# Sums of the seven-product scheme in the first token block: split operands added in PSUM by TensorE through identity weights, instead of by VectorE

## The chip, the cores and the metric

The kernel runs on one core of one Trainium2 chip. The metric is the device time of one execution in microseconds. Before the change three runs took 2962.57, 2964.04 and 2958.99 us, median 2962.57.

## The reference

One layer of a streaming encoder over 2048 prompt rows and 64 sample rows of width 1024: a normalised projection, a convolution and an attention in parallel, a gated merge, an output projection with a residual, then a normalised feed-forward with a residual. The change lies between the output projection and the feed-forward:

```python
x = x + gt1 * (merged @ p['w_o'])
h2 = rms_norm(x, p['norm2_g']) * (1 + sc2) + sh2
gate, up = jnp.split(h2 @ p['w_ffn_in'], 2, axis=-1)
x = x + gt2 * ((jax.nn.silu(gate) * up) @ p['w_ffn_out'])
```

`w_ffn_in` is 1024 x 5632; gate and up have 2816 columns each (22 tiles of 128, called f in the code).

## The kernel before, in words

Everything is float32 carried as two rounded parts, hi and lo (type `fp32r`): a product a*b is three matmuls, hi*hi, hi*lo, lo*hi (`mm3`). A `split` makes the parts: ScalarE (ACT) writes hi by a copy, VectorE (DVE) subtracts it from the source and writes lo.

The second half of the program goes through the token blocks `CBLOCKS`: rows 0 to 576, 576 to 1344, 1344 to 2112. For each block, `merge` makes the merged rows, TensorE (PE) multiplies them by `w_o` into PSUM tiles `pw` (two banks of 512 columns for each 128 rows), `residual` turns each row tile into operands of the feed-forward, and then the products with `w_ffn_in` follow (tiles `ps`, `product`), then those with `w_ffn_out` (tiles `pd`).

The products with `w_ffn_in` use a scheme with seven products in place of eight. The normalised rows, transposed, are cut into four: b11 and b21 are the two halves of the 1024 features for the first half of the block's rows, b12 and b22 the same for the second half. What is multiplied is b11, b21, b22 and the sums

- t3 = b22 - b12
- t1 = b12 - b11
- t2 = b22 - t1
- t4 = b21 - t2

each split into hi and lo. In the first block each half has 288 rows, so these matmuls have 288 columns.

`residual` is a generator, one for each row tile. For one tile of the second half it does: two products with the gate row and two additions of x on DVE (x1), a square with a row sum on ACT, a power on GpSimd (POOL), a scaled copy on ACT (`xn`), eight 128x128 transposes on PE into the tile's own two `pw` banks, eight scalings with shift (`kk` in 0 to 7; the first bank in place, the second into `xn`), by ACT where `kk % 3`, else by DVE; then the sums. There, b[0] is b12 in PSUM (first bank), b[1] is b22 in SBUF (`xn`), t is the second bank. DVE makes t = b22 - b12; subtracts b11 hi and b11 lo from b[0]; makes t = b22 - b[0]; then b[0] = b21 hi - t, + b21 lo. With the splits that is 11 DVE and 5 ACT instructions of 128x512 for a tile.

The row tiles of the first block are 0 (64 sample rows), 64, 192, 320 and 448. Its second chunk, with `last` true, has the tiles 320 and 448; below they are called A and B. `W.early` is true in the first block until its generators are drained.

Order of the work: a recorder (`Meter`, `Stream`) adds estimated nanoseconds for each engine (`Stream.add`) and pumps generators (lanes `turns` and `work`) by these estimates; the weights' splits go to POOL or DVE by them too. Behind it, a scheduler places the instructions of each engine in its queue. Every engine runs its queue in order. While A and B are turned into operands, PE has products that need only b11 and b21: for each of the first five f (`EARLY`) one with b11 (`first`) and one with b21 (`second`) of 12 matmuls each, kept in `early` after a silu. Then come, for f = 0, the products with t3, t2, t1, t4 and b22 in this order (`up`), which need every row tile. `W.get` hands out the weights, loaded by SP's DMA queue, summed by POOL (`ws`), split by ACT (`whi`) and DVE or POOL (`wlo`).

All instructions have line 102 (the recorder's call), so they are told apart by tiles: `pw` the banks of A and B, `b` the tiles b11, b21 and b22 (hi and lo), `t` the tiles t1 to t4, `xn` the normalised rows, `ps` a feed-forward product, `early`, `u`, `v` its kept results, `hid` the hidden rows, `whi`, `wlo` weights.

Of the kernel before, what the change touches and what calls it, by code (L numbers as in the profile page):

```python
# [9 lines left out]
F32R = mybir.dt.float32r  # L10
AF = mybir.ActivationFunctionType
ALU = mybir.AluOpType
# [65 lines left out]
def tile_chunks(lo, hi):  # L78

    tiles = token_tiles(lo, hi)  # L80
    t, n = tiles[(len(tiles) + 1) // 2 - 1]
    return [(lo, t + n), (t + n, hi)]
# [87 lines left out]
class Stream:  # L170
# [7 lines left out]
    def add(self, name, op, n, args, kw):  # L178
        if name == "pe":
            x = args[1]  # L180
            if op == "transpose":
                ns = 128 / 1.2
            elif x.dtype == F32:
                ns = max(n, 64) / (2.4 if "tile_position" in kw else 0.6)
            else:
                ns = (n if n >= 256 else 512) / 2.4
        elif name == "act":
            ns = 220 + 0.83 * n
        elif name == "pool":
            ns = 260.0 * n if ALU.pow in args else 60 + 2.25 * n  # L190
        else:
            fast = op in ("tensor_scalar", "tensor_copy")
            ns = 75 + n * (8.3 if op == "reciprocal" else 0.75 if fast else 1.04)
        self.load[name] = max(self.load[name], self.load["pe"]) + ns
# [423 lines left out]
def streaming_layer(ctx: ExitStack, tc: tile.TileContext, I, O):  # L618
# [1129 lines left out]
    def residual(pp, t, n, gt1, a, half, hs, free, last, i):  # L1748


        which = int(t < SMP)
        if W.early:
            x_t = quarter("x_t", 1, F32, (P, D))
            nc.sync.dma_start(x_t[:n], rows(x_p, x_s, t, n))
            x_t = [x_t[:, 512 * j : 512 * j + 512] for j in range(2)]
        else:
            x_t = [wk.tile([P, 512], F32, tag="ws", name="x_t", bufs=4) for _ in range(2)]
            for j in range(2):
                nc.sync.dma_start(x_t[j][:n], rows(x_p, x_s, t, n)[:, 512 * j : 512 * j + 512])
        yield  # L1760
        x1 = token_row("x1")
        for j in range(2):
            f = slice(512 * j, 512 * j + 512)
            if t < SMP:
                fold(pp[j], x1[:n, f])
            stream.after("dve", "pe")
            dve.tensor_tensor(pp[j][:n], pp[j][:n], gt1[which][:n, f], ALU.mult)
        hs["rows"] -= 1
        yield
        for j in range(2):  # L1770
            f = slice(512 * j, 512 * j + 512)
            dve.tensor_tensor(x1[:n, f], pp[j][:n], x_t[j][:n], ALU.add)
        free()
        yield stream.when("dve")
        xn = token_row("xn")
        ssq = wk.tile([P, 1], F32, tag="ssq", bufs=2)
        act.activation(xn[:n], x1[:n], AF.Square, accum_out=ssq[:n])
        nc.sync.dma_start(x1_d[t : t + n], x1[:n])
        yield stream.when("act")
        r = rsqrt_mean(wk, ssq[:n], n, 1, D, 4)  # L1780

        W.behind = lambda ins=gps.last.ins: tc.issue_after(ins)
        yield stream.when("pool")
        stream.after("act", "pool")
        act.activation(xn[:n], x1[:n], AF.Copy, scale=r)
        yield stream.when("act")

        pts = pp if last else [bank_of(Y[i % 2 * 2 + j], "pt") for j in range(2)]
        pts = [pt.rearrange("p (k n) -> p k n", k=4) for pt in pts]
        for kk in range(KT):  # L1790
            pe.transpose(pts[kk // 4][:, kk % 4, :n], xn[:n, kk * P : (kk + 1) * P], ident[:n, :n])
        cols_ = [pts[0], xn[:, 512:].rearrange("p (k n) -> p k n", k=4) if a + n > half else pts[1]]
        for kk in range(KT):
            g, k = divmod(kk, 4)
            A, B = A2[:, kk, which : which + 1], B2[:, kk, which : which + 1]
            h = cols_[g][:, k, :n]
            if kk % 3:
                stream.after("act", "pe")
                act.activation(h, pts[g][:, k, :n], AF.Identity, bias=B, scale=A)
            else:  # L1800
                stream.after("dve", "pe")
                dve.tensor_scalar(h, pts[g][:, k, :n], A, B, ALU.mult, ALU.add)
        hs["columns"] -= 1
        yield stream.when("dve", "act")
        for c, e, o in ((0, min(n, half - a), a), (max(0, half - a), n, max(0, a - half))):
            if c >= e:
                continue
            b = [x[:, :, c:e] for x in cols_]
            at = lambda name: [hs[name][j][:, :, o : o + e - c] for j in range(2)]
            as_f32 = lambda name: [x.bitcast(F32) for x in at(name)]  # L1810
            if a + c < half:
                for g in range(2):
                    split(*at("b%d1" % (g + 1)), b[g])
                    yield stream.when("dve")
                continue

            yield lambda: not hs["rows"]
            assert not hs["rows"]
            for name in ("t2", "t3", "t1", "t4", "b22"):
                if name not in hs:  # L1820
                    hs[name] = [quarter(name, 1) for _ in range(2)]
            t = pts[1][:, :, c:e]
            stream.after("dve", "act")
            dve.tensor_tensor(t, b[1], b[0], ALU.subtract)
            stream.after("act", "dve")
            act.activation(at("t3")[0], t, AF.Copy)
            act.activation(at("b22")[0], b[1], AF.Copy)
            for x in as_f32("b11"):
                dve.tensor_tensor(b[0], b[0], x, ALU.subtract)
            dve.tensor_tensor(at("t3")[1], t, as_f32("t3")[0], ALU.subtract)  # L1830
            dve.tensor_tensor(t, b[1], b[0], ALU.subtract)
            yield stream.when("dve")
            split(*at("t2"), t)
            split(*at("t1"), b[0])
            yield stream.when("dve")
            dve.tensor_tensor(b[0], as_f32("b21")[0], t, ALU.subtract)
            dve.tensor_tensor(b[0], b[0], as_f32("b21")[1], ALU.add)
            dve.tensor_tensor(at("b22")[1], b[1], as_f32("b22")[0], ALU.subtract)
            yield stream.when("dve")
            split(*at("t4"), b[0])  # L1840
            yield stream.when("act")

    c0, c1 = tile_chunks(*CBLOCKS[0])
    nxt = [first_gates, gate_columns(*c0, 1)]
    srcs = [src]
    W.last_phase(wk, sum_d)
    for s, (lo, hi) in enumerate(CBLOCKS):
# [4 lines left out]
        for i, (c0, c1) in enumerate(chunks):  # L1852
            m = [wk.tile([P, KT, CW // 2], F32R, tag=f"m{j}", name="m") for j in range(2)]
            merge(c0, c1, srcs[i], m, nxt, (lambda: srcs.append(load_mixed(*chunks[1], 1))) if len(srcs) == 1 else None)
            if c1 < hi:
                nxt = [gate_columns(c1, hi, ct) for ct in range(2)]
            else:
                turns.drain(groups[0], True)
            grp = [(t, n) for t, n in tiles if c0 <= t < c1]
            pss = [[row_bank(i, j) for j in range(2)] for i in range(len(grp))]  # L1860
            if not groups:
# [459 lines left out]
```

## Time and profile before

| what | value |
|---|---|
| runs | 2958.99, 2962.57, 2964.04 us |
| profiled execution, its own time | 2963.08 us |
| its span, first to last instruction | 2961.1 us |
| mean granted TensorE clock | 0.997 |
| PE busy | 2892.8 us (98%) |
| DVE busy | 2050.5 us (69%) |
| ACT busy | 1364.9 us (46%) |
| POOL busy | 1155.6 us (39%) |

Times in rows are microseconds from the start of the span. A row of a timeline has start, length, engine, line, operation, out<-in, size, count, and in brackets how long the engine stood idle ahead of it and what it waited for. Rows that follow each other on one engine overlap a little: an instruction starts before the one ahead of it has ended.

### The profile page before, as it was taken

What the parts mean: (1) busy time and instruction counts of PE and PEld (TensorE: products, weight loads), DVE (VectorE), ACT (ScalarE), POOL (GpSimd) and SP (SyncE); (2) the same over time, 40 slices, a digit from 0 to 9 for tenths busy, and PEclk for the clock granted to TensorE, in tenths of its full rate; (3) what the DMA queues carried; (4) which work ended last, traced back from release to release, by engine and by line L of the source; (5) the groups of instructions that cost most, each with busy time, mean ns of one, the idle gap of its engine ahead of it and who ended that gap; (6) DMA issues with size and microseconds to landing.
All of it is one profiled execution on the core that took longest, in us unless ns stands there. A gap on an engine that the chain in (4) does not pass through costs nothing. (4 is left out here: it accounts for less than half of the span.)

```text
span 2961.1 us, 44835 instructions
## 1 busy us (share of the span) xinstructions
PE 2892.8 (98%) x16181; PEld 2584.5 (87%) x16181; DVE 2050.5 (69%) x3662; ACT 1364.9 (46%) x2453; POOL 1155.6 (39%) x747
## 2 busy tenths in 40 slices
PE   8999899999999999989999999999999999999999
PEld 5899777787888788889999998999999999999998
DVE  5897687668857885477777746676666547566666
ACT  3345633661465257464443345444444345444442
POOL 1101310111011102454466452366666742465767
PEclk9999999999999999999999999999999999999999
DMA  9988889988987889885444786333333965323333
GB/s 319 316 290 294 281 286 308 279 260 274 300 275 224 278 251 286 277 284 169 152 153 143 252 262 232 100 113 95 112 122 108 325 229 185 97 95 112 115 103 128
DMA packets 467067, 628.04 MB, mean 212 GB/s; under 512 B 36196, under 2 KB 314584, under 8 KB 466845
## 3 DMA queue, kind: packets, MB, share of 16 engines
q1 hardware_dynamic: 452944, 606.11, 63.2%
q10 hardware_dynamic: 13901, 19.08, 1.8%
q8 instruction: 127, 2.08, 0.3%
q14 instruction: 95, 0.78, 0.1%
HBM read 476.53 MB, written 148.54 MB: 211 GB/s over the span
## 5 line engine op out<-in xcount | busy, mean ns | idle before, releaser
L102 PE MATMUL ps<-t,whi 128*128 128x384 f32 (+1 forms) x2112 | 504.4, 323 | 9.1 <-ACT t L102 2.7
L102 POOL TENSOR_TENSOR wlo<-wst,whi 128x1024 fp32r<-128x1024 f32 (+1 forms) x158 | 361.2, 2298 | 242.8 <-ACT whi L102 217.1
L102 ACT ACTIVATE whi<-wst 128x1024 fp32r<-128x1024 f32 (+1 forms) x266 | 259.0, 978 | 325.5 <-PE ps L102 142.9
L102 PE MATMUL ps<-b,whi 128*128 128x384 f32 (+1 forms) x1584 | 380.2, 325 | 4.5 <-ACT early L102 1.4
L102 PEld LDWEIGHTS ps<-t,whi 128*128 128x128 f32 x2112 | 369.6, 189 | 16.8 <-ACT u L102 3.1
L102 DVE SCALAR_TENSOR_TENSOR y<-u,wd,y 128x512 f32<-128x512 f32 (+1 forms) x480 | 369.3, 773 | 6.3
L102 PE MATMUL ps<-hh,whi 128*128 128x512 f32 (+2 forms) x992 | 360.9, 364 | 0.0
L102 DVE TENSOR_TENSOR acc<-acc,pd 128x512 f32<-128x512 f32 x482 | 322.5, 685 | 49.3 <-PE pd L102 46.8
L102 PE MATMUL ps<-hl,whi 128*128 128x512 f32 (+2 forms) x992 | 344.9, 348 | 0.0
L102 PE MATMUL ps<-hh,wlo 128*128 128x512 f32 (+2 forms) x992 | 344.5, 347 | 0.0
L102 PE MATMUL ps<-t,wlo 128*128 128x384 f32 (+1 forms) x1056 | 339.3, 322 | 0.0
L102 PE MATMUL pd<-whi,hid 128*128 128x512 f32 x912 | 297.2, 391 | 0.3 <-DVE acc L102 0.3
L102 PEld LDWEIGHTS ps<-b,whi 128*128 128x128 f32 x1584 | 276.4, 188 | 12.8 <-ACT early L102 3.1
L102 POOL TENSOR_TENSOR r<-t,mhalf 128x1 f32<-128x1 f32 (+2 forms) x68 | 84.3, 1241 | 448.5 <-DVE t L102 443.5
L102 PE MATMUL ps<-b,wlo 128*128 128x384 f32 (+1 forms) x792 | 255.8, 323 | 0.0
L102 ACT ACTIVATE pr<-pr,sm 128x640 f32<-128x640 f32 (+3 forms) x272 | 200.2, 747 | 109.0 <-DVE sm L102 106.3
L102 PEld LDWEIGHTS ps<-hh,wlo 128*128 128x128 f32 x992 | 186.3, 188 | 21.6
L102 DVE TENSOR_TENSOR wlo<-wst,whi 128x1024 fp32r<-128x1024 f32 (+1 forms) x108 | 135.9, 1262 | 97.7 <-ACT whi L102 94.9
L102 PEld LDWEIGHTS ps<-hh,whi 128*128 128x128 f32 x992 | 186.8, 188 | 18.5 <-issue 1.6
L102 PEld LDWEIGHTS pd<-whi,hid 128*128 128x128 f32 x912 | 171.1, 188 | 36.1 <-DVE acc L102 1.0
L102 PEld LDWEIGHTS ps<-hl,whi 128*128 128x128 f32 x992 | 187.1, 189 | 15.4 <-issue 1.4
L102 PEld LDWEIGHTS ps<-t,wlo 128*128 128x128 f32 x1056 | 199.2, 189 | 0.7
(229 smaller groups left out, 6292.0 us busy)
## 6 DMA issues: line engine op xcount, KB each, us to landing
whi<-w_din_h SPq DMA_DIRECT2D x72, 512.0 KB, 6.8
wlo<-w_din_l SPq DMA_DIRECT2D x72, 512.0 KB, 7.3
wst<-sum_d SPq DMA_DIRECT2D x131, 256.0 KB, 2.9
wfo<-in_w_ffn_out SPq DMA_DIRECT2D x64, 512.0 KB, 3.8
wmod<-in_w_ada SPq DMA_DIRECT2D x46, 512.0 KB, 9.3
sum_d<-ws SPq DMA_DIRECT2D x88, 256.0 KB, 2.1
wst<-in_w_ffn_in SPq DMA_DIRECT2D x85, 256.0 KB, 3.2
wst<-in_w_in SPq DMA_DIRECT2D x40, 512.0 KB, 7.6
```

The lines of the kernel that those rows point to most:

```text
L102: self.last = f(*args, **kw)
```

## The change

Only the tiles A and B of the first block are touched (`by_pe = last and W.early`). For them

- DVE no longer subtracts b11 from b[0], no longer makes t a second time, and no longer combines b21 with t: 5 DVE instructions of 128x512 less for a tile.
- PE adds instead, straight into the PSUM bank, with a 128x128 tile of weights that is the identity or its negative (`signs`) and the hi and the lo part as moving data, 512 columns: b[0] += -b11, t += b11 (so t becomes t2), t += -b21 (so t becomes -t4). That is 3 pairs, 6 matmuls, for a tile.
- t4 is read with the sign turned: hi by an ACT copy with scale -1, lo by one DVE scalar_tensor_tensor.
- The eight transposes of a tile are given as four to an accumulation group (start flag on the first, stop on the fourth), as matmuls with `is_transpose`.
- Of the eight scalings DVE makes four (kk even) and ACT four, before DVE three and ACT five.
- `signs` is made by two ACT copies of the identity ahead of A and B.
- `Stream.add` counts such a transpose as it counted one before.

```diff
-            if op == "transpose":
+            if op == "transpose" or kw.get("is_transpose"):
...
         which = int(t < SMP)
+        by_pe = last and W.early
...
-            pe.transpose(pts[kk // 4][:, kk % 4, :n], xn[:n, kk * P : (kk + 1) * P], ident[:n, :n])
+            dst, src = pts[kk // 4][:, kk % 4, :n], xn[:n, kk * P : (kk + 1) * P]
+            if by_pe:
+                pe.matmul(
+                    dst, src, ident[:n, :n], is_transpose=True, start=kk % 4 == 0, stop=kk % 4 == 3,
+                    skip_group_check=True,
+                )
+            else:
+                pe.transpose(dst, src, ident[:n, :n])
...
-            if kk % 3:
+            if kk % (2 if by_pe else 3):
...
             dve.tensor_tensor(t, b[1], b[0], ALU.subtract)
+            if by_pe:
+                def add(dst, sign, name):
+                    for x in at(name):
+                        pe.matmul(dst, signs[0][:, sign], x, start=False, stop=True, skip_group_check=True)
+
+                split(*at("t3"), t)
+                add(b[0], 1, "b11")
+                yield stream.when("dve")
+                add(t, 0, "b11")
+                split(*at("b22"), b[1])
+                yield stream.when("dve")
+                split(*at("t2"), t)
+                split(*at("t1"), b[0])
+                yield stream.when("dve")
+                add(t, 1, "b21")
+                yield stream.when("dve")
+                act.activation(at("t4")[0], t, AF.Copy, scale=-1.0)
+                stream.after("dve", "act")
+                dve.scalar_tensor_tensor(at("t4")[1], t, -1.0, as_f32("t4")[0], ALU.mult, ALU.subtract)
+                yield stream.when("act")
+                continue
...
+                if not s:
+                    signs.append(wk.tile([P, 2, P], F32R, tag="tg1", name="signs", bufs=2))
+                    for j in range(2):
+                        act.activation(signs[0][:, j], ident, AF.Copy, scale=1.0 - 2.0 * j)
```

What this does to the queues is seen in the order of the instructions. First DVE, before, from the first lo part of t3 to the second one. Tile A has the banks pw_13557 (b[0]) and pw_13558 (t) and the rows xn_13793, tile B pw_13559, pw_13560 and xn_13871; b11 is 12924 and 12925, b21 12926 and 12927.

```order
L102 TENSOR_TENSOR t3_13740<-pw_13558,t3_13739 128x4x128
L102 TENSOR_SCALAR pw_13559<-pw_13559,A2_173,B2_174 128x128
L102 TENSOR_TENSOR pw_13558<-xn_13793,pw_13557 128x512
...
L102 TENSOR_TENSOR t1_13742<-pw_13557,t1_13741 128x4x128
L102 TENSOR_TENSOR pw_13560<-xn_13871,pw_13559 128x512
L102 TENSOR_TENSOR pw_13557<-b21_12926,pw_13558 128x512
L102 TENSOR_TENSOR pw_13559<-pw_13559,b11_12924 128x512
L102 TENSOR_TENSOR pw_13557<-pw_13557,b21_12927 128x512
L102 TENSOR_TENSOR pw_13559<-pw_13559,b11_12925 128x512
L102 TENSOR_TENSOR t3_13740<-pw_13560,t3_13739 128x4x128
```

The same stretch of DVE with the change; A has now the banks pw_13560 and pw_13561, B pw_13562 and pw_13563, and t3 is 13736 and 13737.

```order
L102 TENSOR_TENSOR t3_13737<-pw_13561,t3_13736 128x4x128
L102 TENSOR_TENSOR t1_13739<-pw_13560,t1_13738 128x4x128
L102 TENSOR_SCALAR xn_13915<-pw_13563,A2_173,B2_174 128x128
L102 TENSOR_TENSOR wlo_14009<-ws_13992,whi_14008 128x512
L102 TENSOR_TENSOR t2_13735<-pw_13561,t2_13734 128x4x128
L102 TENSOR_TENSOR pw_13563<-xn_13915,pw_13562 128x512
L102 SCALAR_TENSOR_TENSOR early_13731<-tg_14001,ps_13842 128x288
L102 TENSOR_TENSOR b22_13743<-xn_13915,b22_13742 128x4x128
L102 SCALAR_TENSOR_TENSOR t4_13741<-pw_13561,t4_13740 128x4x128
L102 TENSOR_TENSOR t3_13737<-pw_13563,t3_13736 128x4x128
```

Between B's first subtraction (pw_13560, now pw_13563, from xn) and B's lo part of t3 stood four instructions on the banks of A and B, and now stand a silu's end, a lo part of b22 and A's lo part of t4.

PE before, where the last product with b21 ends and the first with t3 begins (the third row goes to another f):

```order
L102 MATMUL ps_13993<-b21_12927,whi_13770 128x288
L102 MATMUL ps_13993<-b21_12926,wlo_13771 128x288
L102 MATMUL ps_14058<-t3_13739,whi_13846 128x288
L102 MATMUL ps_14171<-t3_13739,whi_14039 128x288
L102 MATMUL ps_14058<-t3_13740,whi_13846 128x288
```

PE with the change: first a place among the products with b21, where A's third pair and B's first pair of additions stand, then the same end of the products as above.

```order
L102 MATMUL ps_13957<-b21_12926,whi_13718 128x288
L102 MATMUL pw_13561<-b21_12926,signs_13557 128x512
L102 MATMUL pw_13561<-b21_12927,signs_13557 128x512
L102 MATMUL ps_13957<-b21_12927,whi_13718 128x288
L102 MATMUL ps_13957<-b21_12926,wlo_13719 128x288
L102 MATMUL pw_13562<-b11_12924,signs_13557 128x512
L102 MATMUL pw_13562<-b11_12925,signs_13557 128x512
...
L102 MATMUL ps_14004<-b21_12926,wlo_13774 128x288
L102 MATMUL ps_14063<-t3_13736,whi_13849 128x288
L102 MATMUL pw_13563<-b11_12924,signs_13557 128x512
L102 MATMUL pw_13563<-b11_12925,signs_13557 128x512
L102 MATMUL ps_14063<-t3_13737,whi_13849 128x288
```

Four of the six pairs stand ahead of the first product with t3, B's second pair behind its first matmul, and B's third pair behind the first matmuls with t2.

Beyond this place the order differs up to the products of f = 8 of the first block (names aside): six splits of weights that DVE made are POOL's, and the first matmuls with `w_ffn_out` come a little earlier on PE. From there on the order is the same.

More of the change, by code (lines that the diff above doesn't have):

```diff
@@ L1841, in residual @@
             yield stream.when("act")
+    signs = []
     c0, c1 = tile_chunks(*CBLOCKS[0])
```

## The prediction

> **What bounds the kernel now.** The page first: the span, the busy shares, the shares of the chain that ended last.
>
> ```profile
> span 2961.1 us, 44835 instructions
> ...
> PE 2892.8 (98%) x16181; PEld 2584.5 (87%) x16181; DVE 2050.5 (69%) x3662; ACT 1364.9 (46%) x2453; POOL 1155.6 (39%) x747
> ```
>
> PE is the bound nearly everywhere: work on another engine counts only where PE stands and waits for it, and every matmul that is added costs its time unless PE would have stood there. So the next view is who PE waited for, from the end of the first block's output projection on (1285 to 1400 us).
>
> ```profile
> PE ps L102 <- ACT t L102: 2.7, 1, 2.7
> PE ps L102 <- DVE u L102: 1.9, 1, 1.9
> PE ps L102 <- DVE t L102: 1.7, 1, 1.7
> ```
>
> Two of the three are waits for the tiles t1 to t4, which the change makes in another way. How much time the place holds is seen in the view by stretches; its columns are the length, the busy time of PE, of its weight load, of DVE, ACT and POOL (with counts), the granted clock, and DMA.
>
> ```profile
> 1306.00:1314.00 8.00, 7.90 (x58) 7.67 (x58) 6.72 (x14) 8.00 (x21) 3.61 (x3) 1.00 1.05 402
> 1314.00:1319.20 5.20, 0.82 (x5) 0.35 (x3) 4.86 (x10) 3.57 (x8) 0.34 (x1) 0.92 0.97 340
> 1319.20:1324.70 5.50, 5.42 (x22) 5.42 (x23) 5.50 (x11) 1.60 (x3) 2.32 (x3) 0.50 0.54 184
> 1324.70:1328.30 3.60, 3.54 (x25) 3.31 (x24) 3.60 (x4) 1.53 (x3) 2.48 (x2) 0.94 0.26 98
> 1328.30:1330.00 1.70, 0.00 (x0) 0.00 (x0) 1.70 (x5) 0.22 (x1) 0.17 (x1) 1.00 0.56 176
> 1330.00:1340.00 10.00, 9.58 (x71) 9.38 (x72) 9.78 (x18) 4.51 (x7) 3.72 (x3) 1.00 0.77 245
> sum 34.00, PE 27.27 PEld 26.14 DVE 32.16 ACT 19.43 POOL 12.63; mean PE 4.54 PEld 4.36 DVE 5.36 ACT 3.24 POOL 2.10
> ```
>
> DVE is busy without a gap from 1314 on, and PE stands: 34.00 - 27.27 = 6.7 us idle. In the third stretch, just behind the long stand, the granted clock is 0.50; PE's 5.42 us there are worth 2.7 us at full clock, so 2.7 us more are lost. **The place holds 9.4 us in all.**
>
> **The place row by row.** PE's timeline (the last 288-column products with b11 or b21, then those with the sums):
>
> ```profile
> 1313.60 0.30 PE L102 MATMUL ps<-b,wlo 128*128 128x288 f32 x1
> ...
> 1313.99 0.29 PE L102 MATMUL ps<-b,wlo 128*128 128x288 f32 x1
> 1317.03 0.53 PE L102 MATMUL ps<-t,whi 128*128 128x288 f32 x2 [2.74 <-ACT t L102]
> 1319.28 0.61 PE L102 MATMUL ps<-t,whi 128*128 128x288 f32 x1 [1.72 <-DVE t L102]
> 1319.68 0.45 PE L102 MATMUL ps<-t,wlo 128*128 128x288 f32 x1
> ...
> 1320.40 0.45 PE L102 MATMUL ps<-t,wlo 128*128 128x288 f32 x1
> ...
> 1330.12 0.50 PE L102 MATMUL ps<-t,whi 128*128 128x288 f32 x2 [1.87 <-DVE u L102]
> ```
>
> Three matmuls take 0.39 us (1313.60 to 1313.99), 0.13 each; behind the wait 0.72 (1319.68 to 1320.40), 0.24 each. DVE at the same time, from A's first subtraction to B's t3:
>
> ```profile
> 1308.72 0.69 DVE L102 TENSOR_TENSOR pw<-xn,pw 128x512 f32<-128x512 f32 x1 [1.11 <-ACT xn L102]
> ...
> 1315.55 0.69 DVE L102 TENSOR_TENSOR pw<-xn,pw 128x512 f32<-128x512 f32 x1
> 1316.15 0.69 DVE L102 TENSOR_TENSOR pw<-b,pw 128x512 f32<-128x512 f32 x1
> 1316.75 1.89 DVE L102 TENSOR_TENSOR pw<-pw,b 128x512 f32<-128x512 f32 x3
> 1318.54 1.28 DVE L102 TENSOR_TENSOR t<-pw,t 128x512 fp32r<-128x512 f32 x2
> ```
>
> B's t3 was subtracted at 1315.55, and its lo part was made at 1318.54 only, behind four instructions with b11 and b21 (1316.15 to 1318.54, 2.4 us). Those four are what the change takes off DVE. One DVE instruction of 128x512 follows the next after 0.60 us (1316.15 to 1316.75).
>
> **What is added to PE.** No row of before shows an addition with identity weights. The nearest are the output projection's matmuls, of the same type and 512 columns:
>
> ```profile
> 1284.62 0.61 PE L102 MATMUL pw<-whi,m 128*128 128x512 f32 x2
> ...
> 1285.30 0.61 PE L102 MATMUL pw<-whi,m 128*128 128x512 f32 x2
> ...
> L102 PE MATMUL pw<-whi,m x528: 387/389/497, 1210.8 to 2463.9; 128*128 128x512 f32 x176
> ```
>
> Three of them take 0.68 us, 0.227 each, and one alone lasts 0.389. Twelve additions cost 12 x 0.227 = **2.7 us**, at the most 12 x 0.389 = 4.7, each standing alone behind a wait. Below nothing it can't be: they are more work on the bound engine. The transposes stay sixteen in number and size; their flags cost nothing.
>
> **When PE runs out of free work.** These rows carry what follows: PE's first product behind the transposes, a scaling and a copy on ACT, a lo part on DVE.
>
> ```profile
> 1306.00 0.53 PE L102 MATMUL ps<-b,whi 128*128 128x288 f32 x2
> L102 ACT ACTIVATE xn<-pw,B,A x24: 452/464/502, 1306.0 to 2482.5; 128x128 f32<-128x128 f32 x24
> L102 ACT ACTIVATE t<-pw x32: 576/597/644, 1309.4 to 2495.8; 128x512 fp32r<-128x512 f32 x32
> L102 DVE TENSOR_TENSOR t<-pw,t x32: 676/682/693, 1311.1 to 2496.4; 128x512 fp32r<-128x512 f32 x32
> ```
>
> Before, the free products end about 1314.1 (1313.99 + 0.13). Now four pairs stand among them, 8 x 0.227 = 1.8 us: they end about 1315.8, if no addition waits.
>
> **Does one wait?** A's first pair stands behind some 18 products counted from 1306.0, at 1308.9; it needs A's first subtraction, which before ended at 1308.72 + 0.69 = 1309.4 and now about 1308.5, because ACT has one scaling less for A. A's second pair, 9 products and a pair later, starts near 1310.5 and is in PSUM at 1311.1; it needs A's lo part of t3, at 1310.2. B's subtraction now waits on a loop over three engines: A's second pair (1311.1), ACT's hi of t2 (0.60, ACT being busy until 1311.4: 1312.0), ACT's last scaling of B behind it (0.46: 1312.4), DVE's subtraction (0.69: 1313.1 to 1313.4). That is still more than 2 us ahead of before, 1315.55 + 0.69 = 1316.2. A's third pair needs A's lo part of t2, near 1312.8, and PE is there near 1312.7; B's first pair follows at 1313.6.
>
> **The waits for t3 and t2.** B's hi of t3 has b22's hi, an `early` copy and A's t4 ahead on ACT: 1314.1 to 1314.7. Its lo part on DVE follows A's t4: 1314.9 to 1315.6. PE asks for them at 1315.8. **The waits of 2.74 and 1.72 us close, with 0.2 us to spare, and with no long stand there is no half clock.** B's second pair then runs from 1315.9; hi of t2 is there at 1317.1, lo at 1317.9; PE, with 11 products of t3 (1.5 us) between, asks for them at 1317.8 and 1318.4. Two instructions that no row shows: the lo part of t4 is now a scalar_tensor_tensor reading PSUM. Its nearest rows are 0.68 for the lo parts above and 0.77 for this:
>
> ```profile
> L102 DVE SCALAR_TENSOR_TENSOR y<-u,wd,y 128x512 f32<-128x512 f32 (+1 forms) x480 | 369.3, 773 | 6.3
> ```
>
> I take 0.69: 0.1 at the most for each tile. The two ACT copies that make `signs` (0.46 each at the most, by the scalings) fall where PE works on the output projection and no wait of PE is listed after 1285 that they could lengthen; nothing. The scalings alternate between ACT and DVE more often, which may cost a hand-over of some 0.1 us each; they lie in the 0.9 us that A gains.
>
> **What is late next.** PE's products with t1 wait until DVE has taken `u` from their bank, the third wait (1.87). From B's first subtraction to `u` DVE needed 1329.53 - 1315.55 = 14.0 us for 21 instructions; now there are 14. Seven at 0.60 to 0.69 are 4.2 to 4.8 us, so `u` starts 9.2 to 9.8 behind 1312.7, at 1321.9 to 1322.5, where PE asks for it at 1321.5 (21 products behind the last pair) and gets it 0.44 later. Weights' splits stand in between, and these rows show what they can cost:
>
> ```profile
> 1324.89 1.54 DVE L102 TENSOR_TENSOR wlo<-ws,whi 128x512 fp32r<-128x512 f32 x1
> ...
> 1329.53 0.44 DVE L102 TENSOR_TENSOR u<-ps,early 128x288 f32<-128x288 f32 x1
> ...
> 1324.60 1.28 POOL L102 TENSOR_TENSOR ws<-ws,wup 128x512 f32<-128x512 f32 x1 [1.20 <-DVE wlo L102]
> ```
>
> The split took 1.54 us beside a sum of weights on POOL, 0.69 elsewhere; it ended 0.55 behind POOL's end. Such hits are in the 14.0 us, and one more or less moves `u` by 0.9. Behind that, the first matmul into `pd`, which now comes earlier, waits for `hid`, for which DVE has a split of 1024 columns ahead. Together these waits are between 0 and 2.5 us (1.0 and 1.5). I take 0.6, nearer to nothing, because the stretch of before up to `u` holds two such hits already and PE's demand comes 2 to 3 us later than DVE would be there without them.
>
> [...]
>
> **What cannot follow.** The weights are bound by DMA up to 1319: POOL's sum for f = 1 waits for a store,
>
> ```profile
> 1318.87 1.28 POOL L102 TENSOR_TENSOR ws<-wfo,ws 128x512 f32<-128x512 f32 x1 [9.18 <-DMA sum_d<-ws]
> ...
> 1340.00:1400.00 60.00, 60.00 (x369) 54.69 (x368) 46.13 (x78) 26.83 (x50) 26.04 (x18) 1.00 0.49 157
> ```
>
> and it will wait as long with the change. Its split is first used with b22 of f = 1, about 1333, so some 10 us are there. In the 60 us behind the place PE is busy without a gap, DVE has 14 us to spare and POOL 34; the six splits that go from DVE to POOL (some 1.3 to 2.6 us each) find room, and I cost the later order at nothing. Were POOL late, the wait would be PE's and start at a wait for `wlo`, which PE never had before.
>
> **The sum**, against the profiled execution's own 2963.08 us: -9.4 (idle and half clock) + 2.7 (additions) + 0.6 (waits left) = -6.1, so 2957.0. The median of the runs is 0.5 lower; for it I forecast 2962.57 - 6.1 = **2956.5 us**. Bounds: all waits closed, the short starts behind them too (four times some 0.3 us), -9.4 - 1.2 + 2.7 = -7.9; additions at 0.389 and waits of 2.5, -9.4 + 4.7 + 2.5 = -2.2.
>
> **The rivals.**
>
> *All closes.* DVE's `u` and `hid` are in time and the short starts go too: -7.9, so 2954.7. For it: PE asks late for everything. Against it: steps 0.2 us wide.
>
> *The half clock was this execution's own.* The 2.7 us come from a clock that halved once, behind 5 us of near idle. The runs lie 5 us apart (2958.99 to 2964.04), so the typical run may not have it. Then the gain is 6.1 - 2.7 = 3.4: 2959.2. [...]
>
> *Half is kept.* Additions alone behind their waits (4.7) and the waits for `u` and `hid` in full (2.5): -2.2, so 2960.4.
>
> *PE parks at the additions: slower.* PE's queue is in order, and the pairs stand ahead of products that need nothing. If ACT and DVE are late, products wait that before ran freely. The three-engine loop (pair, hi on ACT, lo on DVE, next pair) is the place; a turn costs about 0.45 + 0.60 + 0.68 us and ACT's and DVE's queues. It decides from 6.7 us of waiting on (9.4 - 2.7), 1.1 us for each of the six pairs. At 1.5 us each and with the half clock kept: +9.0 + 2.7 + 2.7 - 9.4 = +5.0, so 2967.6. Against it: the pairs' inputs are there 0 to 0.4 us ahead in the steps above. For it: hardly any is ahead by more.
>
> **How the numbers follow.** Forecast 45% (its own range 2955.0 to 2958.0), all closes 22%, clock 10%, half kept 11%, slower 12%. 0.2% is 5.9 us, 2956.65, about what a measurement of this kernel can tell from no change. Faster by more: all closes, and two thirds of the forecast, 52%. Within: the rest of the forecast, clock and half kept, 36%. Slower by more: 12%. The range takes in the three cases on the faster side and the runs' spread of 2 us: 2952.5 to 2962.0; it leaves out the slower case and some of the far ends.
>
> **What the changed profile would show.** PE with twelve matmuls from `signs`, their spacing 0.227; the waits for `t` gone or below 0.5 in sum; the granted clock 1.00 from 1306 to 1340; the wait for `u` below 1; no wait at a matmul into `pw` from `signs` above 0.3. Wrong it would be if PE waits at the additions for DVE `t` or `pw` (the parked queue), if a wait for `wlo` comes up between 1330 and 1500, or if the clock halves again.

## The result, and the profile after

Twelve runs of each kernel: the changed one has a median of 2958.62 us (2956.66 to 2967.0), the one before 2965.26 us (2958.99 to 2970.57). The ratio is 0.998 with a 95% interval of 0.9971 to 0.9989, so 5.9 us were saved (3.3 to 8.6). A later series gave 0.9979 (0.997 to 0.9987), 6.2 us. The forecast was 6.1.

The page of the changed kernel's profiled execution (its own time 2958.2 us):

```profile
span 2956.1 us, 44848 instructions
...
PE 2895.5 (98%) x16193; PEld 2587.1 (88%) x16193; DVE 2041.9 (69%) x3648; ACT 1363.3 (46%) x2453; POOL 1166.4 (39%) x753
```

TensorE (PE) has the 12 matmuls more. VectorE (DVE) has 14 instructions fewer, 3648 against 3662: ten sums and the six splits that went to GpSimd (POOL), less two scalings more. The span is 5.0 us shorter.

What PE waited for between 1306 and 1345 us of the span (the columns: engine, tile it wanted, who was late; us in total, times, longest):

```profile
PE ps L102 <- DVE u L102: 0.9, 1, 0.9
PE pd L102 <- DVE hid L102: 0.3, 1, 0.3
```

The two waits for `t` are gone, the one for `u` went from 1.87 to 0.92. The same place in stretches (busy us of PE, PEld, DVE, ACT, POOL with instructions, then granted clock, share of DMA, GB/s):

```profile
1306.00:1314.00 8.00, 8.00 (x59) 7.59 (x57) 7.43 (x16) 7.85 (x20) 3.85 (x3) 1.00 1.03 379
1314.00:1319.20 5.20, 5.20 (x35) 4.74 (x34) 5.17 (x11) 5.20 (x12) 0.38 (x1) 1.00 0.90 299
1319.20:1324.70 5.50, 4.58 (x33) 4.26 (x32) 5.50 (x8) 1.20 (x4) 3.84 (x4) 1.00 0.58 197
1324.70:1330.00 5.30, 5.30 (x43) 5.30 (x42) 4.17 (x7) 3.41 (x5) 3.82 (x3) 1.00 0.73 221
1330.00:1340.00 10.00, 9.74 (x70) 9.29 (x69) 9.60 (x23) 4.80 (x11) 5.15 (x4) 1.00 0.79 248
```

PE is busy where it waited before, and the granted clock is 1.00 throughout. DVE is as full as it was: 5.17 of 5.20 and 5.50 of 5.50 us in the second and third stretch. Its chain in the timeline (start, length, engine, line, operation):

```profile
1308.95 0.70 DVE L102 TENSOR_TENSOR pw<-xn,pw 128x512 f32<-128x512 f32 x1
...
1314.05 0.69 DVE L102 TENSOR_TENSOR pw<-xn,pw 128x512 f32<-128x512 f32 x1
...
1319.11 2.15 DVE L102 TENSOR_TENSOR wlo<-ws,whi 128x512 fp32r<-128x512 f32 x2
1321.18 0.44 DVE L102 SCALAR_TENSOR_TENSOR early<-tg,ps 128x288 f32<-128x288 f32 x1
1321.54 0.68 DVE L102 SCALAR_TENSOR_TENSOR t<-pw,t 128x512 fp32r<-128x512 f32 x1
1322.14 1.39 DVE L102 TENSOR_TENSOR wlo<-wst,whi 128x512 fp32r<-128x512 f32 x1
1323.45 0.45 DVE L102 TENSOR_TENSOR u<-ps,early 128x288 f32<-128x288 f32 x1
```

From A's first subtraction to `u` it is 1323.45 - 1308.95 = 14.50 us; before it was 1329.53 - 1308.72 = 20.81. And PE:

```profile
1297.51 0.53 PE L102 MATMUL ps<-b,whi 128*128 128x288 f32 x2 [2.05 <-ACT early L102]
...
1310.23 0.63 PE L102 MATMUL pw<-b,signs 128*128 128x512 f32 x2
1310.69 0.42 PE L102 MATMUL ps<-b,whi 128*128 128x288 f32 x2
...
1323.95 0.53 PE L102 MATMUL ps<-t,whi 128*128 128x288 f32 x2 [0.92 <-DVE u L102]
...
1356.26 0.53 PE L102 MATMUL ps<-b,whi 128*128 128x288 f32 x2 [1.40 <-DVE v L102]
```

A pair of additions keeps PE for 10.69 - 10.23 = 0.46 us, 0.23 each. The first row is the last wait that both traces share ahead of the place; in the one before it is

```profile
1297.33 0.54 PE L102 MATMUL ps<-b,whi 128*128 128x288 f32 x2 [0.69 <-ACT early L102]
```

From there to PE's start on t1, behind the wait for `u`, it is 26.44 us after and 1330.12 - 1297.33 = 32.79 us before, 6.35 less. Not all of that is won: in the new order 11 matmuls more stand behind this start (8865 to the end, before 8854), some 1.4 us by the 0.13 that a product takes in the trace of before, an estimate. The order does not matter from that last shared wait to the 8000th matmul before the end, where both queues are alike again. Here is that stretch in the traces of before, of the change and of the change run again (columns as above):

```profile
1297.33:1467.79 170.46, 162.21 (x1023) 150.09 (x1024) 136.27 (x227) 82.19 (x164) 74.99 (x55) 0.98 0.56 186
1297.51:1463.96 166.45, 163.20 (x1034) 151.08 (x1035) 126.50 (x212) 81.34 (x162) 83.11 (x59) 0.99 0.57 186
1294.11:1460.44 166.33, 161.98 (x1034) 149.55 (x1035) 129.76 (x215) 81.49 (x162) 84.06 (x59) 1.00 0.58 191
```

**4.0 us are won at this place** (170.46 - 166.45), and 4.1 in the second trace. PE stood idle for 8.25 us of the stretch before, and for 3.25 and 4.35 us after. The last row of PE's fence is part of what is left: a wait for `v` of 1.40 that was not there before. To the end of the span it is 1658.59 after (2956.1 - 1297.51) and 1663.77 before, 5.2 less; the 1.2 us beyond the 4.0 lie behind the stretch, where the second trace is 1.5 us longer than before, so they are no part of the gain that can be told.

### The profile page after: what moved, and what is told of

Read it like the earlier page. It is cut to its first block, busy times and chain, and to the rows that moved or that the text cites. A ratio compares the mean times of both kernels' runs of the same rounds, so it can differ in the third digit from the quotient of the medians.

```text
span 2956.1 us, 44848 instructions
## 1 busy us (share of the span) xinstructions
PE 2895.5 (98%) x16193; PEld 2587.1 (88%) x16193; DVE 2041.9 (69%) x3648; ACT 1363.3 (46%) x2453; POOL 1166.4 (39%) x753
## 4 chain that ended last, share of the span: by engine, by line
PE 48%; DVE 2%; ACT 1%; issue 1%; DMA 0%; POOL 0%; ACTq 0%; DVEq 0%
PE ps L102 29%; PE pd L102 14%; PE pw L102 5%; DVE wlo L102 1%; DVE pw L102 0%; ACT whi L102 0%; DVE ps L102 0%; DVE t L102 0%; DMA tg<-g_d 0%; DVE sums L102 0%; PE pt L102 0%; DVE acc L102 0%; ACT xn L102 0%; DVE hid L102 0%; ACT hid L102 0%
```

## The experiments

The prediction added up PE's times (waits closed, clock restored, additions charged); call that theory P. Its rival in the first series is theory D: DVE's chain sets when `u` is there, and what PE does ahead of it is covered. Theory Q in the later series is D with what the first had shown. Twelve runs followed, each five rounds beside the kernel before.

| kernel | ratio to before (95%) | splits on DVE between A's first subtraction and u: number, us | that distance, us | PE's waits there, us | the stretch: length; PE idle; lost to half clock (behind the start on t1), us |
|---|---|---|---|---|---|
| before | 1 | 6, 5.98 | 20.81 | t 4.46, u 1.87 | 170.46; 8.25; 2.9 (0) |
| spare matmuls | 1.0005 (0.9995 to 1.0014) | 6, 5.93 | 20.80 | t 1.42, u 3.34 | 174.41; 8.00; 3.2 (1.5) |
| scalings alone | 0.9992 (0.9981 to 1.0002) | 6, 5.94 | 21.82 | t 4.00, u 2.52 | 172.84; 9.47; 4.6 (1.7) |
| B alone | 0.9999 (0.999 to 1.0008) | 6, 7.88 | 20.24 | t 0.84, wlo 0.90, u 4.18 | 174.40; 10.47; 2.5 (2.5) |
| A alone | 1.0004 (0.9995 to 1.0013) | 6, 5.77 | 18.62 | t 0.25, wlo 0.18, u 3.39 | 174.05; 8.36; 4.6 (2.9) |
| b11 alone | 0.9997 (0.9987 to 1.0007) | 6, 5.15 | 17.31 | u 2.38, v 2.23 | 170.99; 9.02; 0 |
| before, splits on POOL | 0.9995 (0.9985 to 1.0004) | 0 | 17.96 | t 4.45 | 169.04; 7.27; 2.9 (0) |
| B alone, splits on POOL | 0.9993 (0.9984 to 1.0001) | 0 | 12.40 | t 0.84, hid 3.01 | 171.04; 8.43; 1.7 (1.7) |
| change | 0.998 (0.9971 to 0.9989) | 5, 4.91 | 14.50 | u 0.92, hid 0.26 | 166.45; 3.25; 1.7 (0) |
| change, again | 0.9979 (0.997 to 0.9987) | 5, 4.20 | 14.04 | u 0.48, hid 1.53 | 166.33; 4.35; 0 |
| change, more matmuls | 0.9993 (0.9983 to 1.0004) | 5, 4.43 | 15.39 | none | 168.54; 3.65; 0 |
| change, 2 splits on POOL | 0.9986 (0.9977 to 0.9995) | 3, 2.04 | 13.11 | hid 0.57 | 165.66; 3.39; 0 |
| change, splits on POOL | 0.9987 (0.9978 to 0.9997) | 0 | 13.47 | pw 0.60, v 0.92, second u 0.85 | 166.10; 3.74; 0 |
| change in all blocks | 0.9991 (0.9982 to 1.0) | 5, 3.31 | 13.64 | pw 0.42, hid 1.42 | 165.86; 3.99; 0 |

An interval is some 2.7 us to either side, so the ratios tell little between neighbours; the columns beside them, from one trace each, tell more. The stretch is the one above, from the 7160th matmul to the 8000th before the end (36 more for the change in all blocks, whose additions stand behind it). A matmul at half clock is charged half of its time as lost (in the trace of before a product took 0.24 us there, 0.13 elsewhere). The stretch orders the kernels much as their medians do: where it took 165.7 to 166.5 us, the medians are 2958.6 to 2961.1 us, and where it took 168.5 or more, 2962.3 to 2966.7. So most of the gain is made here.

**Spare matmuls** in the kernel before:

```diff
                 z = bank("z0")
+                for _ in range(0 if s else 32):
+                    nc.tensor.matmul(z, hs["b11"][0][:, 0, :P], hs["b21"][0][:, 0, :half], start=True, stop=True)
```

> The kernel before, with 32 spare matmuls of 288 columns, inputs ready long before, put on TensorE where it waits for the first product with t3, into the bank that this product starts afresh. They should occupy the two waits at 1314.3 to 1319.3 (2.74 and 1.72 us in the trace of before) without moving what ends them, and so keep the granted clock from halving at 1318. Theory D (VectorE's chain up to u sets the place: u at 1329.5 whatever TensorE does before): the time stays, 0 +- 1 us, and the wait for u grows from 1.9 to about 4.6 us. Rival P (TensorE's time adds up: the half clock costs its 2.7 us, as the prediction's sum has it): 2.7 us faster than before, wait for u as before, about 1.9.

Its PE:

```profile
1317.17 4.12 PE L2001 MATMUL ps<-b,b 128*128 128x288 f32 x30
1322.34 0.40 PE L102 MATMUL ps<-t,whi 128*128 128x288 f32 x1 [0.79 <-DVE t L102]
1325.34 0.40 PE L102 MATMUL ps<-t,whi 128*128 128x288 f32 x1 [0.63 <-DVE t L102]
1333.15 0.82 PE L102 MATMUL ps<-t,whi 128*128 128x288 f32 x2 [3.34 <-DVE u L102]
```

The waits for `t` shrank from 4.46 to 1.42 us, and the wait for `u` grew from 1.87 to 3.34. DVE's distance is the same to 0.01 us, and so is PE's way from A's first subtraction to its start on t1: 1333.15 - 1311.76 = 21.39 us, before 1330.12 - 1308.72 = 21.40. The half clock ahead of `u` was covered by DVE's chain: D. The time alone would not say it. It did not move, and 2.7 us (0.0009) lie outside the interval, but the halving was not avoided: it came back behind the longer wait for `u`, where it cost 1.5 us. In A alone and B alone, below, it stands there too. One stretch behind the start on t1 for each (spare matmuls, A alone, B alone), with PE busy throughout at a granted clock of 0.50:

```profile
1333.15:1336.20 3.05, 3.05 (x13) 3.05 (x14) 2.50 (x4) 0.00 (x0) 1.64 (x2) 0.50 0.70 198
1330.76:1336.60 5.84, 5.84 (x24) 5.84 (x25) 3.90 (x6) 0.63 (x1) 4.37 (x4) 0.50 0.85 254
1331.06:1336.06 5.00, 5.00 (x21) 5.00 (x22) 3.33 (x6) 0.00 (x0) 3.53 (x3) 0.50 0.88 272
```

**Scalings alone**, in the kernel before:

```diff
-            if kk % 3:
+            if kk % (2 if last and early_rows else 3):
```

> The kernel before with one part of the change alone: in the last two row tiles of the first block VectorE makes four of the eight scalings and ScalarE four, instead of three and five. Theory D (VectorE's chain up to u is the bound): VectorE has two more instructions of 0.4 us ahead of u, so 0 to +0.8 us against before. Rival S (the gain of the change comes from ScalarE's scalings, which held up A's first subtraction by the 1.11 us that VectorE waited for ScalarE's xn): 1 us or more faster than before.

No gain that can be told; the ratio is 2.4 us on S's side, but its interval holds 1. The distance is 1.0 us longer, though not for D's reason: both scalings more stand ahead of A's first subtraction, and 33 DVE instructions follow up to `u` as before. Two of them, the lo parts of b22 from `xn`, took 1.25 and 1.47 us in place of 0.68 each.

**One tile alone**, B (tile 448) or A (320):

```diff
-        by_pe = last and W.early
+        by_pe = last and W.early and t == 448
```

> The changed kernel, but only the last row tile (448, B) has its sums made by TensorE; tile 320 (A) is as before. Theory D: five VectorE instructions of 0.60 us fewer between A and u instead of ten, and VectorE has no idle time there, so u comes some 3 us earlier than before and the time is 3 us below before, half of the change's gain. Rival B (only what lies behind B's first subtraction counts, since A's sums lie ahead of it): the whole gain of the change, 5 to 6 us below before, and less than that by nothing but 0.2 us. Rival P (TensorE's own time): six additions fewer than the changed kernel, 1.4 us, so faster than the changed kernel if the waits close all the same.

> The changed kernel, but only row tile 320 (A) has its sums made by TensorE; the last one (448, B) is as before. Theory D: as with B alone, some 3 us below before, and the two halves add up to the whole. Rival B (only B's chain counts): within 1 us of before.

Neither gave anything that can be told. B alone fails all three theories (D's 3 us lie at the very end of its interval); A alone agrees with rival B, which B alone contradicts. DVE behind B's sums, with B alone:

```profile
1321.66 0.69 DVE L102 SCALAR_TENSOR_TENSOR t<-pw,t 128x512 fp32r<-128x512 f32 x1 [0.26 <-ACT t L102]
1322.27 1.28 DVE L102 TENSOR_TENSOR wlo<-ws,whi 128x512 fp32r<-128x512 f32 x2
1323.47 0.45 DVE L102 SCALAR_TENSOR_TENSOR early<-tg,ps 128x288 f32<-128x288 f32 x1
1323.83 3.11 DVE L102 TENSOR_TENSOR wlo<-ws,whi 128x512 fp32r<-128x512 f32 x2
1326.86 0.44 DVE L102 SCALAR_TENSOR_TENSOR early<-tg,ps 128x288 f32<-128x288 f32 x1
1327.22 1.74 DVE L102 TENSOR_TENSOR wlo<-wst,whi 128x512 fp32r<-128x512 f32 x1
1328.89 1.75 DVE L102 TENSOR_TENSOR wlo<-ws,whi 128x512 fp32r<-128x512 f32 x1
1330.56 0.45 DVE L102 TENSOR_TENSOR u<-ps,early 128x288 f32<-128x288 f32 x1
```

The sums end at 1322.3, but `u` stands behind six splits of the weights, and those take 7.88 us. POOL adds weights beside the slow ones, which the last section bears on. Take the splits out of the distance and the halves nearly add up: 14.8 us before, 12.4 with B, 12.9 with A, 9.6 with both. PE stood idle all the same, only later: 4.18 and 3.39 us for `u`. This is theory Q. It leaves one thing out: behind these waits the clock halved (rows above), and PE lost 2.5 us with B alone and 2.9 with A alone where it sets the pace. Before, the halving stood ahead of `u`, where DVE did. So D's 3 us for each half may have been there and gone again; how many executions have that halving is not known.

**Splits on POOL**, in the kernel before, in that with B alone, and in the changed one (there also for the first two splits only, with `key[1] != (0, "s4")`):

```diff
-            late = key[0] in ("up", "fo") and key[1] != (0, "s1") and self.stream.load["pool"] - self.stream.load["pe"] > POOL_BEHIND
+            late = key[0] in ("up", "fo") and not (key[0] == "up" and i in self.first and key[1][0] < 2) and key[1] != (0, "s1") and self.stream.load["pool"] - self.stream.load["pe"] > POOL_BEHIND
```

> The kernel before, sums untouched, but the low parts of the weights for f = 0 and 1 (the splits that VectorE makes between A's first subtraction and u, six of them, 5.98 us in the trace of before) are made by GpSimd, which stands idle for 9 us there. Theory Q (u comes after A's first subtraction by what stands in VectorE's queue between them: 20.8 us in before and in the kernel with spare matmuls, 14.8 us of them sums and scalings, 6.0 us splits): the distance falls to about 15 us and PE starts on t1 some 4 to 5.5 us earlier, so 2.5 to 5.5 us faster than before (the smaller if TensorE, at half clock, asks for u late). Rival A (only the additions on TensorE can shorten it): within 1 us of before. Rival W (GpSimd is then late with its own sums of weights and TensorE waits for wlo): slower than before by 1 us or more, with a wait for GpSimd wlo at the products of f = 1.

> The changed kernel with the same splits on GpSimd: none stands in VectorE's queue between A's first subtraction and u any more. Theory Q: the distance falls from 14.5 to about 10 us, u is in time, and the wait for u (0.92 us in the changed kernel's trace) is gone; TensorE's own work is the bound there. 0.9 to 2.6 us faster than the changed kernel, 6.5 to 8.5 below before. Rival W (GpSimd late): a wait for GpSimd wlo behind, and no gain against the changed kernel or a loss.

> The kernel with TensorE's sums for tile B alone, and the splits for f = 0 and 1 on GpSimd. Alone, the first edit left u at 20.2 us behind A's first subtraction, since six splits of 7.9 us stood in between; the second left it at 18.0 us. Theory Q (VectorE's queue ahead of u adds up): 12.4 to 14 us, as low as in the changed kernel, with half of its additions; 3 to 6 us below before. Rival A (it takes both tiles' additions on TensorE): u stays at 18 us or more and the time within 1.5 us of before.

> The changed kernel with only the first two of the five splits ahead of u given to GpSimd, where it stands idle (1310 to 1318.8), so that its sums of weights behind 1318.8 come as they did. Theory Q: u about 1.3 us nearer to A's first subtraction (13.2 us), the wait for u gone, 0.5 to 1.5 us faster than the changed kernel run beside it. Rival W (what is put ahead of GpSimd's sums comes back as a later wait): no gain, and waits for v, hid or wlo behind u that are longer by as much.

Two distances came as Q said (12.40 where 12.4 to 14 was forecast, 13.11 for 13.2). In the other two DVE had nothing left to do and waited. In the kernel before with the splits on POOL it waited for PE:

```profile
1323.43 0.46 DVE L102 TENSOR_TENSOR u<-ps,early 128x288 f32<-128x288 f32 x1 [2.57 <-PE ps L102]
```

PE came late in it because the waits for `t` (2.73 and 1.72) were as before: there the sums themselves are late, not the splits. And there the half clock (0.50 from 1315.0 to 1321.8, 2.9 us lost) does count: it holds up PE, and PE holds up `u`. In the changed kernel it waited for ACT, which waited for PE's additions, in rows such as

```profile
1320.85 0.69 DVE L102 TENSOR_TENSOR t<-pw,t 128x512 fp32r<-128x512 f32 x1 [0.50 <-ACT t L102]
...
1323.00 0.69 DVE L102 SCALAR_TENSOR_TENSOR t<-pw,t 128x512 fp32r<-128x512 f32 x1 [0.73 <-ACT t L102]
```

so the distance stayed at 13.47 us, not 10: without splits it is, by these rows, the loop of additions over three engines that sets it. The times did not follow the distances, and here Q fell as far as it made `u` the gate. With B alone and the splits on POOL, `u` was in time, and the next gate held:

```profile
1324.59 2.81 DVE L102 TENSOR_TENSOR wlo<-ws,whi 128x512 fp32r<-128x512 f32 x2 [1.00 <-ACT whi L102]
1327.33 0.45 DVE L102 TENSOR_TENSOR ps<-ps,u 128x288 f32<-128x288 f32 x1
1327.81 0.47 DVE L102 TENSOR_TENSOR ps<-ps,early 128x288 f32<-128x288 f32 x1
1328.19 2.07 DVE L102 TENSOR_TENSOR wlo<-wfo,whi 128x1024 fp32r<-128x1024 f32 x1
1330.19 0.51 DVE L102 TENSOR_TENSOR hid<-ps,hid 128x64 fp32r<-128x64 f32 x2
```

```profile
1330.45 0.62 PE L102 MATMUL pd<-whi,hid 128*128 128x512 f32 x1 [3.01 <-DVE hid L102]
```

What DVE did not split ahead of `u` it split ahead of `hid`, again beside POOL's sums (2.81 for two of 0.68), and PE waited 3.01 us there. In the changed kernel the two versions with splits on POOL are not faster than the change run again: rival W. In the stretch their traces are 0.2 to 0.8 us shorter than the change's, too little to tell.

**More matmuls** in the changed kernel, in `add`:

```diff
+                    for e in (1 - sign, sign):
+                        nc.tensor.matmul(dst, signs[0][:, e], at(name)[0], start=False, stop=True, skip_group_check=True)
```

> The changed kernel with two more matmuls for each of the six additions, the hi part added and taken away again: 12 more of 512 columns, 2.7 us of TensorE. Theory Q: TensorE still waits 0.9 us for u, so what it does ahead of u is covered up to that: 1.8 us or less slower than the changed kernel, and the wait for u gone. Rival P (each addition costs its 0.227 us): 2.7 us slower than the changed kernel, the wait for u as it was. Rival C (the additions lie in a chain with ScalarE and VectorE, so each costs more than its own time): over 2.7 us, with waits for t in front of u.

The wait for `u` is gone and no wait for `t` came up in front of it, which speaks against C. The medians lie 3.0 to 3.7 us above the changed kernel's in other series, more than Q's 1.8 and P's 2.7, but with intervals as wide as that; the stretch is 2.1 and 2.2 us longer. Q, P and C are not told apart by it.

**b11 alone**: t4 is made by DVE as before.

```diff
-                add(t, 1, "b21")
...
+                dve.tensor_tensor(b[0], as_f32("b21")[0], t, ALU.subtract)
+                dve.tensor_tensor(b[0], b[0], as_f32("b21")[1], ALU.add)
...
+                split(*at("t4"), b[0])
```

> The changed kernel with b11's two additions on TensorE and b21's sum (t4) on VectorE as before: three VectorE instructions fewer for a tile instead of five, and six splits ahead of u in VectorE's queue, as before, not five. Theory Q: 20.8 less six instructions of 0.60 us, so u stands about 17 us behind A's first subtraction, and the time is 2 to 4 us below before. Rival T (all or nothing, as one tile alone gave nothing): within 1 us of before.

The distance is 17.31 us, as Q said; the time is not, and the trace shows where some of it went: waits for `v` of 1.58 and 0.65 us behind that for `u`.

**All blocks**: `by_pe = last`, with `signs` made anew for each block.

> The change taken to the last row tiles of the other two blocks as well: 36 more additions of 512 columns on TensorE, and as many VectorE instructions fewer for each tile there. In the trace of before TensorE waits only 1.7 us in all at the second block's place and 1.5 us at the third's. Theory Q (additions on TensorE pay only where TensorE stood waiting for VectorE): 36 x 0.227 = 8.2 us added, less at most the 3.2 us of waits: 5 to 8 us slower than the changed kernel. Rival V (VectorE's time is what counts everywhere): faster than the changed kernel.

Slower than the change run beside it by 1.8 us by the medians and 3.6 by the ratios, but the two intervals overlap. The trace says more. In the third block alone, from the 3000th matmul before the end to the last (the 3018th here, with 18 additions behind it), it took 575.75 us, the change run again 573.70; the other twelve traces lie between 573.64 and 574.03. That is 2.0 us for additions of 18 x 0.227 = 4.1. So half of them was covered there: the sign is Q's, its size was too large. PE's idle time fell by 1.1 us (from 1.61 to 0.50); what covered the rest was not followed. The second block cannot be read this way, since its 5000 matmuls differ by 3 us between traces of kernels that are alike there.

**The change again**:

> The changed kernel itself once more, so that the next two stand beside it on one chip, and for a second trace of it. Theory Q: u about 14.5 us behind A's first subtraction, as in the first trace, and no wait of TensorE for t; if the granted clock does not halve ahead of the place (it did in the first trace, at 1298 to 1301), the wait for u is longer by as much, up to 2.6 us, and the time is the same, 5 to 6 us below before.

```profile
1319.21 0.53 PE L102 MATMUL ps<-t,whi 128*128 128x288 f32 x2 [0.48 <-DVE u L102]
...
1327.19 0.50 PE L102 MATMUL pd<-whi,hid 128*128 128x512 f32 x1 [1.53 <-DVE hid L102]
```

The clock did not halve near the place, and the wait for `u` was 0.48 us, not longer; it was `hid` that held PE, by 1.53 us.

## Why the prediction was right

- **The time** was forecast at 2956.5 from a median of 2962.57, 6.1 us less. Measured were 5.9 and 6.2 us less; both medians lie higher than forecast, by 2.7 us (before) and 2.1 us (after), since the three runs known ahead were among the faster ones of before. That the measured saving agrees with the forecast to 0.2 us is luck in part: the place gave 4.0 and 4.1 us in the traces, not 6.1, and where the other 2 us of the measured gain come from stays open (the end of the last section has a candidate).
- **Idle time, 6.73 us**: 1.18 us of it were left (0.92 + 0.26); the sum had 0.6. In the second trace it was 2.0 (0.48 + 1.53). Both lie at the two gates that the prediction names, `u` and `hid`, and within its 0 to 2.5. With the wait for `v`, which it does not name, 2.6 and 3.4 us were left. This is the term that was too small: in the stretch idle time and half clock together fell by 6.2 and 6.8 us, not by 9.4 - 0.6 = 8.8. (DVE was not quite without a gap from 1314 on, as the prediction has it: 0.34 us ahead of 1314.35 are a wait for ACT.)
- **The additions, 2.7 us**: twelve of 0.23 us each; none waited in the changed kernel for more than 0.2 us. The sixteen transposes of A and B, given without groups before and in groups after, lasted 0.27 us each (median) in both traces. The rival of the parked queue didn't come; with one tile alone it did in small, as one wait of 0.55 us.
- **DVE's chain**: from B's first subtraction to `u` 9.2 to 9.8 us were forecast, and it took 1323.45 - 1314.05 = 9.40. The times themselves came some 1 to 1.6 us later than forecast, in a trace that lost time ahead of the place (2.05 us of waiting and the halving below).
- **The half clock, 2.7 us, is the term that was wrong in kind.** The sum took it as time that comes back once PE has work. The spare matmuls gave PE work in the same place, and PE started on t1 no earlier: it waited for `u` the longer, and the halving moved behind that wait. The waits at `t`, the half clock and the wait at `u` are one interval that ends at `u`, and `u` came 6.3 us nearer. What may have helped is that no halving followed behind `u`: in these traces one stands at or behind every wait for `u` or `hid` of 2.5 us and more (2.52 to 4.18), and behind none of the shorter ones (2.38 at the most). Ahead of the place the change's trace has one behind a wait of 2.05 us, so the length does not decide alone. The rival by which the gain would be 3.4 where the clock had not halved rests on the same error. The changed kernel's first trace has a halving of its own just ahead of the place (granted clock 0.56 here):

```profile
1297.50:1301.40 3.90, 3.89 (x18) 3.89 (x19) 1.59 (x6) 3.26 (x8) 3.81 (x5) 0.56 0.99 342
```

  It lost 1.7 us of PE's time (half of 3.4), and PE still came to `u` 0.92 us too early.
- **The later order, costed at nothing**: it cost a little. Behind the place both traces of the change have a wait for `v` of 1.40 us. Three splits stand ahead of `v` on DVE; in the trace of before it was two, of 1.97 us in all. The change's rows:

```profile
1352.17 3.67 DVE L102 TENSOR_TENSOR wlo<-ws,whi 128x512 fp32r<-128x512 f32 x3 [8.65 <-ACT whi L102]
1355.76 0.45 DVE L102 TENSOR_TENSOR v<-ps,v 128x288 f32<-128x288 f32 x1
```

  The kernel before has a wait of 0.8 us for ACT's `s` further on that the changed one lacks. From the start on t1 to the end of the stretch PE was idle for 2.3 us after and 1.65 before.

What the prediction did not see is how little room there was: neither tile's additions, nor b11's alone, bring a part of the gain that can be told. What DVE saves is taken by the splits that wait in its queue, until enough of its work is gone that `t`, `u`, `v` and `hid` are all nearly in time; and where a wait for `u` of 2.52 to 4.18 us was left, half clock behind it took 1.5 to 2.9 us more. That this holds because DVE's and POOL's work together fills the place is argued from the traces; no kernel was run that takes the splits themselves away, or that keeps the clock up behind `u` with one tile alone, so neither part is shown by itself.

## What to carry to other kernels

Where an engine is full over a stretch, several waits of another engine in a row are one debt: price the work ahead of the last of them, and don't add up the waits and the clock one by one. Look also at the clock behind the wait that is left (granted at 0.50 in the three stretches of the experiments above). Moving work to the engine that waits pays as far as that engine stood idle, and not much further (in the third block it cost 2.0 us of 4.1). Before splitting a change in parts, look at what stands next in the relieved engine's queue: it takes the room first.

## What the runs showed of the hardware that was not expected

DVE instructions with both inputs in SBUF took up to 1.1 us longer beside an instruction of POOL, though not all of them did. Between 1200 and 1400 us of the trace of before, the 17 splits of 128x512 on DVE that no POOL instruction overlaps took 0.67 to 0.70 us; of the 18 that POOL overlaps by more than 0.1 us, 15 took 0.85 to 1.78 and three 0.68 to 0.69. DVE's instructions of this size with `pw` (PSUM) among their inputs took 0.68 to 0.70, 21 of them with such an overlap. The longer times are measured; their cause is not shown. A small shift went with the difference in the pair that follows. The kernel before and the one with spare matmuls are the same program up to 1312 us. Of before, POOL and DVE:

```profile
1296.54 1.28 POOL L102 TENSOR_TENSOR wlo<-wst,whi 128x512 fp32r<-128x512 f32 x1 [0.61 <-ACT whi L102]
```

```profile
1297.60 0.37 DVE L102 TENSOR_TENSOR b<-xn,b 128x128 fp32r<-128x128 f32 x1
```

and of the one with spare matmuls:

```profile
1298.16 1.29 POOL L102 TENSOR_TENSOR wlo<-wst,whi 128x512 fp32r<-128x512 f32 x1
```

```profile
1298.18 1.43 DVE L102 TENSOR_TENSOR b<-xn,b 128x128 fp32r<-128x128 f32 x1
```

The same instruction took 0.37 us where it started 0.2 us ahead of the end of POOL's split (the next one started at 1297.77), and 1.43 us where it started 0.02 us behind the start of one. Both times it ended 0.15 us behind the end of that split. PE's next wait there was 1.83 us, a halving followed (1302.0 to 1305.5, three matmuls in 0.72 us, behind it in 0.40), and A's first subtraction came 3.0 us later (1311.76 - 1308.72). Waits of 1.34 to 1.83 us at this point stand in seven of the twelve experiments' traces and in neither trace of before and after. They are the seven in which this instruction took 1.41 to 1.43 us; in the other seven it took 0.27 to 0.40 us, and PE waited 0.39 us at the most. These waits may be part of the runs' spread of 10 us, and of the 2 us of gain that the place does not account for, though no run here shows that.
